# Attention heads taken in pairs: two halves of the array's rows for the logits, two halves of its columns for the weighted values

## The chip, the cores and the metric

The kernel runs on one core of a Trainium2 chip. A core has a matrix engine (TensorE, "PE" in the profile, its weight loads "PEld"), a vector engine (VectorE, "DVE"), an activation engine (ScalarE, "ACT"), a general engine (GpSimd, "POOL") and a queue engine (SyncE, "SP") that issues DMAs. TensorE multiplies a stationary operand, loaded into its array of 128 rows by 128 columns, with a moving operand that is streamed through it, and writes to PSUM, which has eight banks. The metric is the time of one execution in microseconds (us); smaller is better.

## What is computed

The reference is a transformer block (two kinds of attention, then a layer of product-key experts) followed by a second block. 256 tokens pass through both. The change lies in the attention of the first block alone: 16 heads of "forgetting" attention (fox) and 16 heads of "dilated" attention (dil), each head 64 wide. Cut to what matters:

```python
# fox: 16 heads of 64, S = 256, in two query blocks of 128
logits = einsum('bhqd,bhkd->bhqk', q * 64 ** -0.5, k) + (c[..., :, None] - c[..., None, :])
p = softmax(where(k_pos <= q_pos, logits, -inf))
o = einsum('bhqk,bhkd->bhqd', p, v)
...
# dil: three windows and dilations, mixed by their log-sum-exp; over 256 tokens this is
# one causal softmax whose logits get log(count) added, the count of patterns that hold the pair
out = concat([rms_norm(fox_o, fox_out_gain), rms_norm(dil_o, dil_out_gain)])
h = x + out @ w_out
```

The causal mask leaves 3 of 4 blocks of 128 by 128 logits for each head: block t = 0 has 128 keys, block t = 1 has 256.

## The kernel before, in words

All big products run in float32r (weights split into a high and a low half, three matmuls for each product), with weights streamed from memory: `Stream` brings 1 MB units by DMA, ACT rounds a half (line 74), DVE subtracts to get the low half (line 75), and PE uses it in `fm` (lines 105 to 107, 256 moving columns) or `tm` (lines 123 to 125, 512 moving columns). Splitting runs three halves ahead of the unit in use, with five half buffers.

The attention stage runs such products one after another: values, keys and queries of fox, then queries, keys and values of dil, then the output projection `w_out` in two halves of four chunks. Work of other kinds, the attention of single heads above all, is put between units of this stream: a list `k.bg` of steps, of which `pump` takes one after each unit (in the first half of `w_out` two in a row). The order on each engine is the program's order; no scheduler changes it.

`attention` makes 18 steps, and runs once for fox (on the units of `w_fq` and `w_dil`) and once for dil (on the last units of `w_dil` and on the first half of `w_out`). Step i holds three parts:

- `s1(i)`, the logits of head i: for fox a bias (line 278, two matmuls of 16 rows and 384 moving columns), then q times k (line 283: 64 rows, moving 128 and 256 columns, float32). An even head has rows 0 to 63 of the array, an odd head rows 64 to 127. Then the softmax: DVE reduces (line 289), ACT takes exp (line 293), DVE inverts and scales (lines 295 and 298) into the tile `lg`.
- `s3(i-1)`, three transposes of the probabilities of the head before (line 305), which ACT copies to `et` (line 307).
- `s4(i-2)`, the weighted values of the head before that (lines 316 and 317: 128 rows, 64 columns of the array, moving 256 and 128 columns, float32). An even head has columns 0 to 63, an odd head columns 64 to 127 of the same PSUM bank. After an odd head `on_pair` splits the pair's result (ACT line 221, DVE line 222), squares it (ACT line 450) and adds the square up (POOL line 451).

PSUM tiles of the tag `bg` rotate through four banks: one for a head's logits, one for its transposes, one for a pair's weighted values. Between these steps stands `rope_T` (line 509: eight transposes of rotated queries or keys, which wait for POOL's rotation, lines 496 to 501).

Of the kernel before, what the change touches and what calls it, by code (L numbers as in the profile page):

```python
# [9 lines left out]
F32 = mybir.dt.float32  # L10
# [5 lines left out]
AF = mybir.ActivationFunctionType  # L16
OP = mybir.AluOpType
# [8 lines left out]
BIG = 1e30  # L26
# [123 lines left out]
def bank(k, tag):  # L150
    return k.p_ps.tile([128, 512], F32, name=tag, tag=tag)
# [15 lines left out]
def pump(k, n=1):  # L167

    for _ in range(n):
        k.tick += 1  # L170
        for f in k.due.pop(k.tick, ()):
            f()
        if k.bg:
            k.bg.popleft()()
# [12 lines left out]
def step(us, f):  # L187
    f.us = us
    return f


def drain(k):
    while k.bg or k.due:
        pump(k)
# [19 lines left out]
def split(k, hi, lo, src, gain=None):  # L214

    nc = k.nc
    if gain is None:
        nc.scalar.copy(hi, src)
        nc.vector.tensor_sub(lo, src, hi.bitcast(F32))
    else:  # L220
        nc.scalar.mul(hi, src, gain)
        nc.vector.scalar_tensor_tensor(lo, src, gain, hi.bitcast(F32), op0=OP.mult, op1=OP.subtract)  # L222
# [44 lines left out]
def attention(k, bias, qT, kT, v, mask, on_pair):  # L267


    nc = k.nc  # L270
    E, ET, OTp = {}, {}, {}

    def s1(h):
        g, e = h // 2, (h % 2) * 64
        ps = bank(k, "bg")
        if bias:
            for i in range(2):
                nc.tensor.matmul(ps[:, :384], bias[1][:, h:h + 1].to_broadcast([16, 128]), bias[0][:, i, :],
                                 start=i == 0, stop=False)
        for t in range(2):  # L280
            o = ps[:, :128] if t == 0 else ps[:, 128:384]
            n = 128 * (t + 1)
            nc.tensor.matmul(o, qT[e:e + 64, g, t * 128:(t + 1) * 128], kT[e:e + 64, g, :n],
                             start=not bias, stop=not bias or t == 1)
        lg = k.p_at.tile([128, 384], F32, name="lg", tag="lg")
        st = k.p_at.tile([128, 6], F32, name="st", tag="st")
        for t in range(2):
            s = slice(0, 128) if t == 0 else slice(128, 384)
            nc.vector.tensor_tensor_reduce(lg[:, s], ps[:, s], mask[:, s], 1.0, BIG, op0=OP.add,
                                           op1=OP.min, accum_out=st[:, t:t + 1])  # L290
        for t in range(2):
            s = slice(0, 128) if t == 0 else slice(128, 384)
            nc.scalar.activation(lg[:, s], lg[:, s], AF.Exp, bias=st[:, t:t + 1], scale=-1.0,
                                 accum_out=st[:, 2 + t:3 + t])
        nc.vector.reciprocal(st[:, 4:6], st[:, 2:4])
        for t in range(2):
            s = slice(0, 128) if t == 0 else slice(128, 384)
            nc.vector.tensor_scalar_mul(lg[:, s], lg[:, s], st[:, 4 + t:5 + t])
        E[h] = lg

    def s3(h):
        ps = bank(k, "bg")
        e = E.pop(h)
        for b in range(3):
            nc.tensor.transpose(ps[:, b * 128:(b + 1) * 128], e[:, b * 128:(b + 1) * 128], k.ident)
        et = k.p_at.tile([128, 384], F32, name="et", tag="et")
        nc.scalar.copy(et, ps[:, :384])
        ET[h] = et

    def s4(h):  # L310
        g, e = h // 2, (h % 2) * 64
        et = ET.pop(h)
        if h % 2 == 0:
            OTp[g] = bank(k, "bg")
        o = OTp[g][e:e + 64, :256]
        nc.tensor.matmul(o, v[:, 0, h * 64:(h + 1) * 64], et[:, :256], start=True, stop=False)
        nc.tensor.matmul(o[:, 128:256], v[:, 1, h * 64:(h + 1) * 64], et[:, 256:384],
                         start=False, stop=True)
        if h % 2:
            on_pair(g, OTp.pop(g))  # L320

    def step(i):
        if i < 16:
            s1(i)
        if 0 <= i - 1 < 16:
            s3(i - 1)
        if 0 <= i - 2 < 16:
            s4(i - 2)
    return [lambda i=i: step(i) for i in range(18)]


def phase_attn(k, A):
    nc, st = k.nc, k.stream
    with ExitStack() as ctx:
# [41 lines left out]
        for c in range(2):  # L376
            accs = [[bank(k, ("acc", "bg")[c]) for t in range(2)] for s in range(2)]
            for q in range(4):
# [12 lines left out]
                for s in range(2):  # L391
                    tm(k, [a[:, :260] for a in accs[s]], w, k.act, q * 4, q == 0, q == 3,
                       n=260, off=s * 260, pitch=520, final=s == 1)
# [10 lines left out]
            for c in range(2):  # L404
                for s in range(2):
                    o = c * 520 + s * 260
                    n = min(260, 1024 - o)
                    for t in range(2):
                        acc = fv_acc[c][s][t]
                        nc.scalar.mul(fv[:, t, o:o + n], acc[:, :n], r[:, t:t + 1])  # L410
                        if n < 260:
                            nc.vector.scalar_tensor_tensor(zf[:, t, :], acc[:, n:260], r[:, t:t + 1],
                                                           fb, op0=OP.mult, op1=OP.add)
# [29 lines left out]
        def on_pair(o, sq, goff):  # L443
            def f(g, ps):
                split(k, o[0][:, g, :], o[1][:, g, :], ps[:, :256], k.gn[:, goff + g:goff + g + 1])
                if g == 0:
                    nc.scalar.activation(sq, ps[:, :256], AF.Square)
                else:
                    s = k.p_at.tile([128, 256], F32, name="sqt", tag="sqt")
                    nc.scalar.activation(s, ps[:, :256], AF.Square)  # L450
                    nc.gpsimd.tensor_add(sq, sq, s)
            return f
# [17 lines left out]
        for s in range(3):  # L470
            for c in range(2):
                accs = [bank(k, "acc") for t in range(2)]
                for q in range(4):
                    tm(k, accs, st.next(), k.act, q * 4, q == 0, q == 3)
                    if s == 2 and c == 0 and q == 2:
                        drain(k)
                        oD = [p1.tile([128, 8, 256], F32R, name="oD%d" % i, tag=("qkA", "qkB")[i]) for i in range(2)]
                        k.bg.extend(attention(k, None, dqT, dkT, dv, msk[:, M_D:M_D + 384],
                                              on_pair(oD, sqD, G_DIL)))
                    if q < 3:  # L480
                        pump(k)
                if s == 2:
                    for t in range(2):
                        nc.scalar.mul(dv[:, t, c * 512:(c + 1) * 512], accs[t], r[:, t:t + 1])
                    pump(k)
                    continue
                rp = k.p_at.tile([128, 2, 512], F32, name="rp", tag="rp", bufs=1)
                for t in range(2):
                    nc.scalar.mul(rp[:, t, :], accs[t], r[:, t:t + 1])
                for t in range(2):  # L490
                    hv = rp[:, t, :].rearrange("p (h e) -> p h e", e=64)
                    x1, x2 = hv[:, :, 0:8], hv[:, :, 8:16]
                    cb = cosv[:, t, None, :].to_broadcast([128, 8, 8])
                    sb = sinv[:, t, None, :].to_broadcast([128, 8, 8])
                    tt = [k.p_at.tile([128, 8, 8], F32, name="rt%d" % i, tag="rt%d" % i) for i in range(4)]
                    nc.gpsimd.tensor_mul(tt[0], x1, cb)
                    nc.gpsimd.tensor_mul(tt[1], x2, sb)
                    nc.gpsimd.tensor_mul(tt[2], x2, cb)
                    nc.gpsimd.tensor_mul(tt[3], x1, sb)
                    nc.gpsimd.tensor_sub(x1, tt[0], tt[1])  # L500
                    nc.gpsimd.tensor_add(x2, tt[2], tt[3])
                pump(k)

                def rope_T(rp=rp, c=c, dst=dkT if s == 1 else dqT, sc=1.0 if s == 1 else -0.125):
                    for q in range(2):
                        ps = bank(k, "bg")
                        for e in range(2):
                            for t in range(2):
                                nc.tensor.transpose(ps[:, e * 256 + t * 128:e * 256 + (t + 1) * 128],
                                                    rp[:, t, (q * 2 + e) * 128:(q * 2 + e + 1) * 128], k.ident)  # L510
                        nc.scalar.mul(dst[:, c * 4 + q * 2:c * 4 + q * 2 + 2, :].rearrange("p g t -> p (g t)"), ps, sc)
                k.bg.appendleft(rope_T)
# [12 lines left out]
        for half in range(2):  # L525
# [5 lines left out]
            o, rr = (oF, rF) if half == 0 else (oD, rD)  # L531
# [1223 lines left out]
```

## Time and profile before

| what | value |
|---|---|
| time, median of 3 runs | 2669.52 us (2668.6 to 2669.95) |
| the profiled execution's own time | 2668.61 us |
| its span on the core | 2666.8 us |
| PE busy | 2621.0 us (98%) |
| PE weight loads busy | 2395.4 us (90%) |
| DVE busy | 1850.6 us (69%) |
| ACT busy | 1438.8 us (54%) |
| POOL busy | 797.9 us (30%) |
| mean granted TensorE clock | 0.995 of full speed |

A float32 matmul stands in the trace as two records, here called passes, each with a weight load of its own; a transpose and a float32r matmul stand as one. The record of a matmul is longer than what it costs: records overlap, since the next one starts while the last one still drains. So time on PE is read here from the start of one row to the start of the next. In the timeline, rows of one line that follow each other are merged: the start of the first, the time to the end of the last, and "x" the number of passes.

### The profile page before, as it was taken

The numbers are of one execution on the slowest core, as the hardware profiler recorded it, in microseconds if no ns is written. First come the engines' busy times: TensorE is split into PE (matmuls) and PEld (weight loads), VectorE is DVE, ScalarE is ACT, GpSimd is POOL, SyncE is SP. The second block draws the span as 40 slices with busy tenths as digits, with TensorE's granted clock in tenths as the row PEclk, the third lists the DMA queues.
The fourth block names the chain that finished last, engine by engine and source line by source line (L and its number), as shares of the span: only waits on it lengthen the run. The fifth ranks groups of instructions, "written<-read, shape, count | busy, mean of one in ns | idle before, by whom it ended". The sixth has DMA issues, their size and how long they took to land. (4 is left out here: it accounts for less than half of the span.)

```text
span 2666.8 us, 45194 instructions
## 1 busy us (share of the span) xinstructions
PE 2621.0 (98%) x18008; PEld 2395.4 (90%) x18008; DVE 1850.6 (69%) x2679; ACT 1438.8 (54%) x2462; POOL 797.9 (30%) x858
## 2 busy tenths in 40 slices
PE   8999999999999999999999999999999999999997
PEld 8977778999999999999988888887999999999886
DVE  5554455799888899979856666665577765555555
ACT  6344455444466666647645555555665544444453
POOL 0001010432200033457645655634255530000000
PEclk9999999999999999999999999999999999999999
DMA  7533435446666688999968888775544446555553
GB/s 291 176 120 138 158 111 174 168 169 211 212 227 232 245 309 312 321 317 321 323 229 292 288 297 295 290 257 189 174 160 156 143 162 205 187 185 186 187 196 120
DMA packets 93975, 582.36 MB, mean 218 GB/s; under 512 B 12288, under 2 KB 12416, under 8 KB 32704
## 3 DMA queue, kind: packets, MB, share of 16 engines
q1 hardware_dynamic: 53696, 381.05, 41.1%
q0 software_dynamic: 35312, 183.46, 19.3%
q10 hardware_dynamic: 4752, 14.92, 1.5%
q8 instruction: 143, 2.34, 0.4%
q14 instruction: 72, 0.59, 0.1%
HBM read 532.19 MB, written 47.19 MB: 217 GB/s over the span
## 5 line engine op out<-in xcount | busy, mean ns | idle before, releaser
L75 DVE TENSOR_TENSOR whl<-raw,whl 128x1024 fp32r<-128x1024 f32 (+2 forms) x917 | 1186.2, 1306 | 585.3 <-ACT whl L74 560.9
L74 ACT CAST whl<-raw 128x1024 fp32r<-128x1024 f32 (+2 forms) x917 | 952.9, 1048 | 657.6 <-PE acc L107 330.9
L107 PE MATMUL acc<-act,whl 128*128 128x256 f32 x3840 | 1076.7, 280 | 3.5 <-DVE whl L75 3.5
L105 PE MATMUL acc<-act,whl 128*128 128x256 f32 x3840 | 1077.8, 281 | 0.2
L106 PE MATMUL acc<-act,whl 128*128 128x256 f32 x3840 | 1075.4, 280 | 0.4
L107 PEld LDWEIGHTS acc<-act,whl 128*128 128x128 f32 x3840 | 728.3, 190 | 3.9 <-DVE whl L75 3.9
L105 PEld LDWEIGHTS acc<-act,whl 128*128 128x128 f32 x3840 | 722.9, 188 | 2.3 <-issue 1.2
L106 PEld LDWEIGHTS acc<-act,whl 128*128 128x128 f32 x3840 | 723.6, 188 | 1.0 <-DVE act L222 1.0
L1160 PE MATMUL acc<-whl,hh 128*128 128x512 f32 x864 | 218.3, 396 | 0.0
L1160 PE MATMUL bg<-whl,hh 128*128 128x512 f32 x864 | 218.1, 396 | 0.0
L123 PE MATMUL acc<-whl,act 128*128 128x512 f32 (+1 forms) x512 | 198.3, 387 | 7.0 <-ACT whl L74 6.9
L124 PE MATMUL acc<-whl,act 128*128 128x512 f32 (+1 forms) x512 | 196.4, 384 | 4.1 <-DVE whl L75 4.1
L1160 PEld LDWEIGHTS bg<-whl,hh 128*128 128x128 f32 x864 | 162.2, 188 | 39.6
L1160 PEld LDWEIGHTS acc<-whl,hh 128*128 128x128 f32 x864 | 162.2, 188 | 39.5
L125 PE MATMUL acc<-whl,act 128*128 128x512 f32 (+1 forms) x512 | 196.1, 383 | 0.8 <-DVE act L222 0.8
L1085 POOL DMA_INDIRECT raw<-in_up,idx_l x100 | 137.0, 1370 | 136.6 <-DVE hh L911 76.9
L123 PEld LDWEIGHTS acc<-whl,act 128*128 128x128 f32 x512 | 97.7, 191 | 29.4 <-ACT whl L74 7.4
L124 PEld LDWEIGHTS acc<-whl,act 128*128 128x128 f32 x512 | 97.5, 190 | 24.7 <-DVE whl L75 5.9
L125 PEld LDWEIGHTS acc<-whl,act 128*128 128x128 f32 x512 | 97.4, 190 | 20.3 <-DVE act L222 1.0
L1085 POOL DMA_INDIRECT hr<-hm_d,idx_l x100 | 103.3, 1033 | 30.5 <-issue 30.5
L742 POOL DMA_DIRECT2D g_d<-gst x16 | 8.8, 551 | 291.9 <-DVE gst L726 291.9
L893 POOL TENSOR_TENSOR ght<-ght,gt 128x512 f32<-128x512 f32 x46 | 76.9, 1673 | 44.2 <-DMA ght<-gh_d 43.7
(405 smaller groups left out, 3176.1 us busy)
## 6 DMA issues: line engine op xcount, KB each, us to landing
raw<-in_down SPq DMA_DIRECT2D x128, 1024.0 KB, 5.8
raw<-in_w_cv SPq DMA_DIRECT2D x32, 1024.0 KB, 4.8
raw<-in_w_gg SPq DMA_DIRECT2D x32, 1024.0 KB, 4.8
raw<-in_w_dil SPq DMA_DIRECT2D x24, 1024.0 KB, 4.8
gt<-g_d POOLq DMA_DIRECT2D x34, 512.0 KB
raw<-in_w_out SPq DMA_DIRECT2D x16, 1024.0 KB, 4.8
raw<-in_w_pq SPq DMA_DIRECT2D x16, 1024.0 KB, 4.9
g_d<-gst POOLq DMA_DIRECT2D x16, 1024.0 KB
```

The source lines that it names most:

```text
L74: nc.scalar.copy(hi[:, s], r[:, s])
L75: nc.vector.tensor_sub(lo[:, s], r[:, s], hi[:, s].bitcast(F32))
L105: k.nc.tensor.matmul(acc, hi[:, f], x, start=j == 0, stop=False)
L106: k.nc.tensor.matmul(acc, hi[:, f], y, start=False, stop=False)
L107: k.nc.tensor.matmul(acc, lo[:, f], x, start=False, stop=j == nk - 1)
L123: k.nc.tensor.matmul(accs[t], ah[:, kk, ts], hi[:, m], start=st, stop=False)
L124: k.nc.tensor.matmul(accs[t], ah[:, kk, ts], lo[:, m], start=False, stop=False)
L125: k.nc.tensor.matmul(accs[t], al[:, kk, ts], hi[:, m], start=False, stop=sp)
L742: nc.gpsimd.dma_start(g_d[g], x.rearrange("p i t -> p (i t)"))
L893: nc.gpsimd.tensor_mul(x, x, gt[:, (j % 2) * 4:(j % 2) * 4 + 4])
L1085: nc.gpsimd.indirect_dma_start(out=out, out_offset=None, in_=table, in_offset=bass.IndirectOffsetOnAxis(ap=idx, axis=0), bounds_check=n - ...
L1160: nc.tensor.matmul(accs[2 * s + c][t], x[:, ts], y[:, c * 512:(c + 1) * 512], start=i == 0 and x is hh and y is hi, stop=last_ and i == N - 1)
```

## The change

`attention` now makes 19 steps over pairs g of heads (2g and 2g+1).

- An even step i = 2g takes the weighted values of pair g-2 (`outputs`) and then the logits of pair g (`logits`). An odd step i = 2g+3 takes the transposes of pair g (`turn`).
- In `logits` each head of the pair has a PSUM bank of its own. Both biases come first, then q times k of both heads for t = 0, then of both heads for t = 1, so that rows 0 to 63 and rows 64 to 127 alternate from one matmul to the next. The softmax of one head, then of the other, follows, operation by operation as before.
- In `outputs` both heads of the pair write to one bank as before; the two matmuls of 256 moving columns stand together, then the two of 128, so that columns 0 to 63 and columns 64 to 127 alternate.
- `lg` has four buffers in place of two. In return the tile `sqt` of `on_pair` and the four tiles `rt0` to `rt3` of the rotation have one buffer in place of two.

The number of matmuls, transposes and operations of the other engines is the same. Nothing outside the attention stage differs.

The new lines of `attention` (the lines that they replace are in the listing above) and the two changes of buffers:

```diff
+    E, ET = {}, {}
+    parts = (slice(0, 128), slice(128, 384))
+
+    def logits(g):
+
+        ps = [bank(k, "bg") for _ in range(2)]
+        if bias:
+            for e in range(2):
+                for i in range(2):
+                    nc.tensor.matmul(ps[e][:, :384], bias[1][:, 2 * g + e:2 * g + e + 1].to_broadcast([16, 128]),
+                                     bias[0][:, i, :], start=i == 0, stop=False)
+        for t in range(2):
+            for e in range(2):
+                es = slice(64 * e, 64 * e + 64)
+                nc.tensor.matmul(ps[e][:, parts[t]], qT[es, g, t * 128:(t + 1) * 128], kT[es, g, :128 * (t + 1)],
+                                 start=not bias, stop=not bias or t == 1)
+        for e in range(2):
+            lg = k.p_at.tile([128, 384], F32, name="lg", tag="lg", bufs=4)
...
+            E[2 * g + e] = lg
+
+    def turn(g):
+        for h in (2 * g, 2 * g + 1):
+            ps = bank(k, "bg")
+            e = E.pop(h)
+            for b in range(3):
+                nc.tensor.transpose(ps[:, b * 128:(b + 1) * 128], e[:, b * 128:(b + 1) * 128], k.ident)
+            ET[h] = k.p_at.tile([128, 384], F32, name="et", tag="et")
+            nc.scalar.copy(ET[h], ps[:, :384])
+
+    def outputs(g):
+
         ps = bank(k, "bg")
...
+        et = [ET.pop(2 * g + e) for e in range(2)]
+        for b, (o, s) in enumerate(((slice(0, 256), slice(0, 256)), (slice(128, 256), slice(256, 384)))):
+            for e in range(2):
+                h = 2 * g + e
+                nc.tensor.matmul(ps[64 * e:64 * e + 64, o], v[:, b, h * 64:(h + 1) * 64], et[e][:, s],
+                                 start=b == 0, stop=b == 1)
+        on_pair(g, ps)
 
     def step(i):
...
+        if i % 2 == 0:
+            if 0 <= i - 4 < 16:
+                outputs((i - 4) // 2)
+            if i < 16:
+                logits(i // 2)
+        elif 0 <= i - 3 < 16:
+            turn((i - 3) // 2)
+    return [lambda i=i: step(i) for i in range(19)]
...
-                    s = k.p_at.tile([128, 256], F32, name="sqt", tag="sqt")
+                    s = k.p_at.tile([128, 256], F32, name="sqt", tag="sqt", bufs=1)
...
-                    tt = [k.p_at.tile([128, 8, 8], F32, name="rt%d" % i, tag="rt%d" % i) for i in range(4)]
+                    tt = [k.p_at.tile([128, 8, 8], F32, name="rt%d" % i, tag="rt%d" % i, bufs=1) for i in range(4)]
```

How this moves PE's work shows in the order of its instructions. In fox, while `w_fq` and `w_dil` stream, PE has between two units before, for each head (`cT` and `id_131` make the bias, `fkT` and `fqT` are keys and queries, `cst` is the identity, `lg` the probabilities, `et` their transposes, `fv` the values, `acc` rows are the stream's):

```order
L107 MATMUL acc<-act_81,whl 128x256
L278 MATMUL bg<-cT,id_131 128x384 x2
L283 MATMUL bg<-fkT,fqT 128x128
L283 MATMUL bg<-fkT,fqT 128x256
L305 MATMUL bg<-cst,lg 128x128 x3
L316 MATMUL bg<-et,fv 64x256
L317 MATMUL bg<-et,fv 64x128
L105 MATMUL acc<-act_81,whl 128x256
```

And with the change, at the same place, for each pair (the new lines are 280 for the bias, 285 for q times k, 306 for the transposes, 317 for the weighted values):

```order
L317 MATMUL bg<-et,fv 64x256 x2
L317 MATMUL bg<-et,fv 64x128 x2
L280 MATMUL bg<-cT,id_131 128x384 x4
L285 MATMUL bg<-fkT,fqT 128x128 x2
L285 MATMUL bg<-fkT,fqT 128x256 x2
L123 MATMUL acc<-whl,act_81 128x512
...
L306 MATMUL bg<-cst,lg 128x128 x6
```

The row of 128 columns and that of 64 columns, which stood once between any two units, now stand twice in a row between every second two, and the transposes have a place of their own between units.

In dil, on the first half of `w_out`, where two steps run in a row (`dkT`, `dqT`, `dv` are keys, queries and values), PE has before:

```order
L283 MATMUL bg<-dkT,dqT 128x128
L283 MATMUL bg<-dkT,dqT 128x256
L305 MATMUL bg<-cst,lg 128x128 x3
L316 MATMUL bg<-et,dv 64x256
L317 MATMUL bg<-et,dv 64x128
```

twice over between two units, and with the change once:

```order
L125 MATMUL acc<-whl,oF_674 128x512
L317 MATMUL bg<-et,dv 64x256 x2
L317 MATMUL bg<-et,dv 64x128 x2
L285 MATMUL bg<-dkT,dqT 128x128 x2
L285 MATMUL bg<-dkT,dqT 128x256 x2
L306 MATMUL bg<-cst,lg 128x128 x6
L123 MATMUL acc<-whl,oF_673 128x512
```

The weighted values moved ahead of the logits, and the transposes behind them.

## Rows read from the trace of the kernel before

**Rows 1.** The page: span, and each engine's busy time, share and instructions.

```profile
span 2666.8 us, 45194 instructions
PE 2621.0 (98%) x18008; PEld 2395.4 (90%) x18008; DVE 1850.6 (69%) x2679; ACT 1438.8 (54%) x2462; POOL 797.9 (30%) x858
```

**Rows 2.** Attention stage: us; PE, PEld, DVE, ACT, POOL busy (instructions); clock; DMA share; GB/s.

```profile
113.00:413.00 300.00, 299.94 (x1497) 228.61 (x1496) 152.66 (x333) 144.96 (x289) 31.56 (x74) 1.00 0.39 135
```

**Rows 3.** Waits of PE's weight loads, 113 to 413 us: us, times, longest.

```profile
PEld bg L509 <- POOL rp L501: 0.4, 1, 0.4
```

**Rows 4.** Timeline of PE, one fox step: start, us, engine, line, operation, passes.

```profile
130.11 0.28 PE L107 MATMUL acc<-act,whl 128*128 128x256 f32 x1
130.32 0.61 PE L278 MATMUL bg<-cT,id 16*128 16x384 f32 x2
130.86 0.92 PE L283 MATMUL bg<-fkT,fqT 64*128 64x128 f32 x4
131.71 0.55 PE L305 MATMUL bg<-cst,lg 128*128 128x128 f32 x3
132.19 0.65 PE L316 MATMUL bg<-et,fv 128*64 128x256 f32 x2
132.67 0.38 PE L317 MATMUL bg<-et,fv 128*64 128x128 f32 x2
132.98 0.39 PE L105 MATMUL acc<-act,whl 128*128 128x256 f32 x1
133.20 0.28 PE L106 MATMUL acc<-act,whl 128*128 128x256 f32 x1
133.32 0.28 PE L107 MATMUL acc<-act,whl 128*128 128x256 f32 x1
```

**Rows 5.** Timeline of PE: eight transposes between matmuls of 128 rows and columns.

```profile
206.22 1.03 PE L509 MATMUL bg<-cst,rp 128*128 128x128 f32 x8
...
207.33 0.39 PE L124 MATMUL acc<-whl,act 128*128 128x512 f32 x1
```

**Rows 6.** Timeline of PE's weight loads, the same fox step.

```profile
130.86 0.52 PEld L283 LDWEIGHTS bg<-fkT,fqT 64*128 64x128 f32 x4 [0.25 <-issue]
...
132.18 0.19 PEld L316 LDWEIGHTS bg<-et,fv 128*64 128x64 f32 x2 [0.17 <-issue]
```

**Rows 7.** Timeline of PE: two dil steps in a row.

```profile
349.47 0.40 PE L124 MATMUL acc<-whl,oF 128*128 128x512 f32 x1
349.70 0.40 PE L125 MATMUL acc<-whl,oF 128*128 128x512 f32 x1
350.03 0.92 PE L283 MATMUL bg<-dkT,dqT 64*128 64x128 f32 x4
...
353.00 0.64 PE L305 MATMUL bg<-cst,lg 128*128 128x128 f32 x3
...
354.71 0.39 PE L124 MATMUL acc<-whl,oF 128*128 128x512 f32 x1
```

**Rows 8.** Timeline of all engines: dil's last two heads, one after the other.

```profile
401.02 0.48 ACT L307 COPY et<-bg 128x384 f32<-128x384 f32 x1 [2.12 <-PE bg L305]
...
401.34 0.38 PE L317 MATMUL bg<-et,dv 128*64 128x128 f32 x2
401.55 0.19 PEld L316 LDWEIGHTS bg<-et,dv 128*64 128x64 f32 x2
401.55 0.65 PE L316 MATMUL bg<-et,dv 128*64 128x256 f32 x2
```

**Rows 9.** Timelines of DVE and ACT: softmax of one dil head, and a pair's end.

```profile
350.99 0.29 DVE L289 CUSTOM_DVE_ANT_0 lg<-bg,amsk 128x128 f32<-128x128 f32 x1 [1.27 <-PE bg L283]
...
353.11 0.29 DVE L289 CUSTOM_DVE_ANT_0 lg<-bg,amsk 128x128 f32<-128x128 f32 x1
...
354.75 0.47 ACT L221 ACTIVATE oD<-bg,gn 128x256 fp32r<-128x256 f32 x1
355.84 0.39 ACT L450 ACTIVATE sqt<-bg 128x256 f32<-128x256 f32 x1 [0.61 <-DVE oD L222]
```

More of the change, by code (lines that the diff above doesn't have):

```diff
@@ L270, in attention @@
     nc = k.nc
-    E, ET, OTp = {}, {}, {}
-    def s1(h):
-        g, e = h // 2, (h % 2) * 64
-        ps = bank(k, "bg")
[L276 to L320, printed above, removed]
@@ L322, in step @@
-    def step(i):
[L323 to L329, printed above, removed]
+    E, ET = {}, {}
[14 more added lines that the diff above has]
+            lg = k.p_at.tile([128, 384], F32, name="lg", tag="lg", bufs=4)
+            st = k.p_at.tile([128, 6], F32, name="st", tag="st")
+            for t, s in enumerate(parts):
+                nc.vector.tensor_tensor_reduce(lg[:, s], ps[e][:, s], mask[:, s], 1.0, BIG, op0=OP.add,
+                                               op1=OP.min, accum_out=st[:, t:t + 1])
+            for t, s in enumerate(parts):
+                nc.scalar.activation(lg[:, s], lg[:, s], AF.Exp, bias=st[:, t:t + 1], scale=-1.0,
+                                     accum_out=st[:, 2 + t:3 + t])
+            nc.vector.reciprocal(st[:, 4:6], st[:, 2:4])
+            for t, s in enumerate(parts):
+                nc.vector.tensor_scalar_mul(lg[:, s], lg[:, s], st[:, 4 + t:5 + t])
+            E[2 * g + e] = lg
```

## The prediction

> **What bounds the kernel now.** I read the page first: PE is busy for 98% of the span, but its records overlap, so that alone proves little [rows 1]. The busy times of the attention stage, 113 to 413 us, say more: PE 299.94 of 300 us at a granted clock of 1.00, DVE and ACT half idle, the DMAs at 0.39 [rows 2]. In the list of waits of the same stretch no matmul of attention waits for another engine by more than some tenths; the one wait with a cause outside attention is 0.4 us for POOL's rotation [rows 3]. So PE's own sequence sets the pace there, and what shortens it should shorten the run. The timeline gives the price of that sequence, read from start to start.
>
> A fox step costs 133.20 - 130.11 - 2 x 0.12 = 2.85 us beyond the stream's matmuls (spaced 0.12) [rows 4]. Its parts come out with three prices:
>
> - A float32 pass of 128 moving columns takes 0.11 us: the eight transposes take 207.33 - 206.22 less one matmul of the stream (0.23), and 0.88 / 8 = 0.11 [rows 5, 7]. One of 256 takes 0.215: (132.67 - 132.19 - 0.05) / 2, where 0.05 is a weight load of 64 columns, from two loads of some 0.14 within 0.19 [rows 4, 6].
> - Weight loads of 128 columns follow each other by 0.11: four in 0.52, the last 0.19 long [rows 6]. Within a group they hide under the pass before.
> - Where the shape of the tile used changes (all rows, 16 rows, 64 rows, 64 columns), the next group starts 0.09 late (from 130.11 to 130.32 is 0.21, against 0.12), and its first weight load is no longer hidden: 0.11 for 128 columns, 0.05 for 64 columns and for a transpose [rows 4, 6]. The eight transposes among the stream's matmuls, of the same shape, pay neither [rows 5].
>
> With these the step is 0.09 + 0.54 (bias) + (0.11 + 0.22 + 0.43 + 0.09) + (0.05 + 0.33 + 0.09) + (0.05 + 0.43 + 0.22 + 0.09) + 0.10 = 2.83, against 2.85 read: 1.95 of passes and 0.90 for five changes of shape.
>
> **What the change removes.** Passes stay the same in number. Changes of shape become fewer. In fox two steps pay 10 for a pair, 1.80 us. After it, the even step pays columns (0.14), 16 rows (0.21), 64 rows (0.20) and back (0.19), together 0.74; the transposes stand alone among matmuls of their own shape and pay nothing. That is 1.06 us for a full pair. Counted step by step, since the ends of the pipeline differ: before, 14 full steps at 0.90 and the first and last two at 0.60, 0.55, 0.33 and 0.33, together 14.4; after, six full even steps at 0.74, two with logits alone at 0.60 and two with outputs alone at 0.33, together 6.3. Saved: **8.1 us**.
>
> In dil there is no bias. Before: two first steps (0.39, 0.34), four single ones at 0.67, five double ones at 1.15 and the last at 0.33, together 9.5. After: two logits steps at 0.39, one with both at 0.53, five double ones at 0.14 + 0.20 + 0.14 = 0.48, then 0.28 and 0.33, together 4.3. Saved 5.2. As a test, a double step by these prices is 2 x 1.63 + 1.15 = 4.41; the trace has 354.71 - 349.70 - 2 x 0.23 = 4.55 [rows 7]. The surplus is in the second transposes (0.64 us for three, where fox shows 0.55): they need the softmax of the head whose logits have just run [rows 4, 7]. Afterwards that softmax has a unit of the stream to finish in. Five of these, 0.1 each: 0.5. Dil saves **5.7 us**, and both together 13.8.
>
> **What the change adds.** The two halves of the array now alternate, a thing that the trace never shows with data ready. A pair's q times k is 8 passes, 4 x 0.11 + 4 x 0.215 = 1.30 us one after the other; the weighted values of a pair are 1.30 too. Bounds: they add up as before (saving 0), or passes of one half run beside those of the other. Each matmul is two passes in the same half, and PE starts in program order, so only the second pass of one head can run beside the first of the next: 8 parts of 0.108 in place of 12, a saving of 0.43 for either block. For the rows the weight loads are a limit: eight of 128 columns, 0.11 apart, as long as the short passes themselves, which leaves 10 parts of 12, a saving of 0.21. Loads of 64 columns, 0.05 apart, limit nothing [rows 6].
>
> The nearest row is at the end of dil, where the weighted values of head 14 (columns 0 to 63) and of head 15 (64 to 127) follow each other [rows 8]. The last pass of the first starts at 401.34 + 0.11 = 401.45 and streams until 401.56; the weight load of the other half starts at 401.55, just after its data came (the copy ends at 401.02 + 0.48 = 401.50). A change of shape would have held it until 401.65. So a change of half doesn't drain the array, and a load goes into one half while the other streams. Whether two halves also stream together it doesn't show, since the data came too late. I take it that they do, because nothing but the order of starts ties them, and take the lower figure for the rows: 0.43 + 0.21 = 0.64 a pair, 16 pairs, **10.2 us**. Ends: 0 and 16 x 0.86 = 13.8.
>
> [...]
>
> **What hides the rest.** On DVE and ACT the operations are the same, in another order: two softmaxes in a row, 2 x (353.11 - 350.99) = 4.2 us [rows 9], in which DVE does no splitting of weights. Splits are three halves, over 8 us of PE, ahead, and DVE's mean load is half, so this costs nothing. The probabilities are wanted a full unit (5.5 us) later. In dil's double steps the second head's transposes need the bank of the weighted values just written, free after ACT's split, DVE's and the square: 355.84 + 0.39 - 354.75 = 1.5 us [rows 9], plus 0.3 to start. PE covers 0.2 + 0.2 + 1.3 + 0.14 + 0.33 without overlap, 1.9 or 1.7 with it; at worst 0.2 x 5 = 1 us, which I leave to the range. A rotation before which only transposes stand has 0.66 us more time than the one that waited 0.4 [rows 3], so it adds no wait. The single buffers for `sqt` and `rt` are taken again on the same engine, or two units later: nothing.
>
> **The sum.** 13.8 + 10.2 = 24.0 us. The profiled execution took 2668.6 (span 2666.8 and 1.8 around it), 0.9 under the median of 2669.5. So 2644.6 on its own time, **2645.5** for the median.
>
> **Rivals.** *The halves don't stream together* (the change doesn't do what it says): only the shape changes are saved, 2669.5 - 13.8 = 2655.7. For it: no row shows two float32 passes at once. Against: the load into the other half. *Only one block overlaps*: columns alone 2648.8, rows alone 2652.3. *Both halves stream all the time*: each block falls from 1.30 to 0.65, which saves 13.8 + 16 x 1.30 = 34.6 and gives 2634.9; against it speaks that the two passes of a matmul share their half and that PE starts in order. [...] *Slower: each alternation drains as a change of shape does.* Three in the rows at 0.20 and three in the columns at 0.14 make 1.02 us a pair, 16.3 in all, against the 13.8 saved: 2672.0, slower than before. It decides from 13.8 / 96 = 0.14 us for an alternation. Rows 8 speak against it for the columns; for the rows nothing is shown, and there alone it would be 9.6 us, not enough to lose. For this to reach beyond measurement, waits of other engines must come on top.
>
> **How the numbers follow.** Overlap in both, 24 to 27.6 us: 0.50. One block only: 0.14. None: 0.26. Full halves: 0.03. Draining halves: 0.05. Waits that nobody saw: 0.02. The range runs from full overlap, 2641.9 less 3 us for prices read to 0.01 us, to no overlap, 2655.7 plus 1 us for the banks: 2639 to 2657, holding the first three. A measurement of this kernel can tell about 0.2%, 5.3 us: faster by more 0.93 (the first four cases), the same 0.05, slower 0.02.
>
> **What would show it.** In the timeline of the changed kernel a full fox pair, outputs and logits together, should take 4.0 us without overlap and 3.4 with it, and its transposes 0.66. Overlap shows in the starts: the first pass of the second head beside the second pass of the first, and the block of lines 285 and 317 shorter than 1.3 us. If the starts of line 285 lie 0.2 apart at each change of head, the halves drain. PE should still have no wait on DVE or ACT; a wait of the transposes for line 450 would make the prediction too low. It is wrong as a whole if another engine, freed of nothing, turns out to hold PE back once PE needs 8% less time in this stage.

## The result and the profile after

The changed kernel takes 2633.6 us (2632.74 to 2634.49), against 2669.06 of the kernel before in the same runs; the ratio is 0.9876, interval 0.9864 to 0.9887. That is 35.5 us less, where 24 were forecast, and 5.4 us below the range. The direction was right, the size was not.

The page of the changed kernel shows the same work in a shorter span (against [rows 1]):

```profile
span 2630.9 us, 45199 instructions
PE 2585.7 (98%) x18008; PEld 2378.6 (90%) x18008; DVE 1846.4 (70%) x2679; ACT 1439.2 (55%) x2462; POOL 788.4 (30%) x858
```

The stage that was 113 to 413 us [rows 2] now ends at 381.4. Busy time by stretch, columns as there (PE, PEld, DVE, ACT, POOL, clock, DMA share, GB/s):

```profile
113.00:381.40 268.40, 267.15 (x1498) 214.00 (x1497) 149.42 (x333) 144.86 (x289) 33.57 (x74) 1.00 0.44 151
```

It holds the same operations, 31.6 us shorter, and PE is still what never stops: 267.15 of 268.40 us.

Where the time went is in the timeline of PE, for a pair of fox heads (start, us, engine, line, operation, passes; [rows 4] has the same for one head):

```profile
142.66 0.28 PE L107 MATMUL acc<-act,whl 128*128 128x256 f32 x1
142.87 0.87 PE L317 MATMUL bg<-et,fv 128*64 128x256 f32 x8
143.67 0.96 PE L280 MATMUL bg<-cT,id 16*128 16x384 f32 x4
144.55 0.93 PE L285 MATMUL bg<-fkT,fqT 64*128 64x128 f32 x8
145.41 0.38 PE L105 MATMUL acc<-act,whl 128*128 128x256 f32 x1
145.63 0.28 PE L106 MATMUL acc<-act,whl 128*128 128x256 f32 x1
```

Read from start to start: the eight passes of q times k take 145.41 - 144.55 = 0.86, of which 0.11 is the first weight load and 0.09 the way out. That leaves 0.66 for passes that are 1.30 one after the other. The weighted values take 143.67 - 142.87 = 0.80, less 0.05 and 0.09: 0.66 again. Both blocks are at half. The whole step costs 145.63 - 142.66 - 2 x 0.12 = 2.73 us where 3.4 was forecast with overlap.

How they come to half shows where a window is opened on the first 0.1 us of the weighted values alone, PE and its weight loads:

```profile
142.86 0.20 PEld L317 LDWEIGHTS bg<-et,fv 128*64 128x64 f32 x4
142.87 0.44 PE L317 MATMUL bg<-et,fv 128*64 128x256 f32 x2
```

Two passes together last 0.44 us, no longer than one record alone (0.43), so they are the first passes of the two heads, and start within 0.01 us of each other; four weight loads fit in 0.20. The prediction had let only the second pass of one head run beside the first of the next.

One place got worse, and eats 2.2 us. In dil's double steps PE now waits for a bank (timeline of all engines, beside [rows 7] and [rows 9]):

```profile
325.94 0.87 PE L317 MATMUL bg<-et,dv 128*64 128x256 f32 x8
...
326.74 0.93 PE L285 MATMUL bg<-dkT,dqT 64*128 64x128 f32 x8
326.86 0.47 ACT L221 ACTIVATE oD<-bg,gn 128x256 fp32r<-128x256 f32 x1 [2.50 <-PE bg L317]
327.37 0.48 DVE L222 SCALAR_TENSOR_TENSOR oD<-bg,gn,oD 128x256 fp32r<-128x256 f32 x1 [1.73 <-ACT oD L221]
...
327.60 0.55 PE L306 MATMUL bg<-cst,lg 128*128 128x128 f32 x3
...
327.95 0.38 ACT L450 ACTIVATE sqt<-bg 128x256 f32<-128x256 f32 x1 [0.61 <-DVE oD L222]
...
328.38 0.31 PEld L306 LDWEIGHTS bg<-cst,lg 128*128 128x128 f32 x3 [0.48 <-ACT sqt L450]
```

The second head's transposes need the bank that held the pair's weighted values; split, subtraction and square read it one after the other until 328.33, and the transposes start at 328.38. In the list of waits of 113 to 385 us this is the largest with a cause:

```profile
PEld bg L306 <- ACT sqt L450: 2.4, 5, 0.5
...
PEld bg L509 <- POOL rp L501: 0.8, 2, 0.4
```

### The profile page after: what moved, and what is told of

Its sections match the earlier page's. It is cut to its first block, busy times and chain, and to the rows that moved or that the text cites. A ratio compares the mean times of both kernels' runs of the same rounds, so it can differ in the third digit from the quotient of the medians.

```text
span 2630.9 us, 45199 instructions
## 1 busy us (share of the span) xinstructions
PE 2585.7 (98%) x18008; PEld 2378.6 (90%) x18008; DVE 1846.4 (70%) x2679; ACT 1439.2 (55%) x2462; POOL 788.4 (30%) x858
## 5 line engine op out<-in xcount | busy, mean ns | idle before, releaser
L1085 POOL DMA_INDIRECT raw<-in_up,idx_l x100 | 130.1, 1301 | 145.4 <-DVE hh L911 78.0
```

The costliest lines, as they stand in the source:

```text
L1085: nc.gpsimd.indirect_dma_start(out=out, out_offset=None, in_=table, in_offset=bass.IndirectOffsetOnAxis(ap=idx, axis=0), bounds_check=n - ...
```

## The experiments

Unless said otherwise, each is an edit of the changed kernel, and is compared with its attention stage: steps of 2.74 us (fox, even), 0.66 (transposes alone) and 2.92 (dil, double), each beyond the stream's own matmuls.

**Do the halves matter, or only the order?** The logits of both heads on the same rows:

```diff
-                es = slice(64 * e, 64 * e + 64)
+                es = slice(0, 64)
```

> The changed kernel, but the logits of both heads of a pair are taken from rows 0 to 63 (so the odd head's logits are those of the even head: that part of the computation is left out). Order, banks and sizes unchanged. If the gain of the block is the two halves of the rows, q times k takes 8 passes one after the other, 1.30 us in place of 0.65: 16 x 0.65 = 10.4 us more, less the wait of dil's double steps (0.43 x 5 = 2.2): 2641.8. Rival (two banks or the alternation of independent matmuls suffice): 0.65 as before, 2633.6.

Measured: 2643.74 us (2640.91 to 2649.53), 2641.8 expected. Timeline of PE, a pair of fox heads:

```profile
146.45 0.96 PE L280 MATMUL bg<-cT,id 16*128 16x384 f32 x4
147.34 1.57 PE L285 MATMUL bg<-fkT,fqT 64*128 64x128 f32 x8
148.84 0.39 PE L105 MATMUL acc<-act,whl 128*128 128x256 f32 x1
```

The block takes 1.50 us in place of 0.86, so the eight passes take 1.30, the sum that the prediction had for no overlap. Two banks and alternating matmuls give nothing; two halves of the rows give all of the block's gain. Double steps come to 3.12, not 2.92 + 0.64: the longer block hides the wait for the bank again. The rival falls. The columns have no such run of their own. For them the evidence is the timeline: the same bank is written before and after, and the eight passes take 0.66 in place of 1.30.

**Does the order matter?** Both blocks head by head, without alternation:

```diff
-        for t in range(2):
-            for e in range(2):
+        for e in range(2):
+            for t in range(2):
...
-        for b, (o, s) in enumerate(((slice(0, 256), slice(0, 256)), (slice(128, 256), slice(256, 384)))):
-            for e in range(2):
+        for e in range(2):
+            for b, (o, s) in enumerate(((slice(0, 256), slice(0, 256)), (slice(128, 256), slice(256, 384)))):
```

> The changed kernel with both blocks written head by head: both matmuls of head 2g (t = 0, 1 or the two of the weighted values), then both of head 2g+1. Same pairs, same number of shape changes, no alternation. In the trace of the changed kernel an alternating block of eight passes takes 0.65 us. Theory A (each half of the array runs its own matmul with its two passes; matmuls are handed out in program order, and one waits only for its own half): q times k 0.22 + 0.22 + 0.43 = 0.87, weighted values 0.43 + 0.43 + 0.22 = 1.08 us; the wait of dil's double steps (0.43 x 5) goes: 2633.6 + 16 x 0.65 - 2.2 = 2641.8. Rival B (a queue for each half, order without weight): blocks stay 0.65, 2633.6. Rival C (passes in program order, as the prediction had it): 1.08 and 1.19, 2633.6 + 16 x 0.97 - 2.2 = 2647. Rival D (no overlap without alternation): 1.30 each, 2652.

Measured: 2635.7 us (2634.67 to 2639.17); the attention stage ends at 382.20, against 381.96 with alternation. The block of line 285 is as long as there:

```profile
144.55 0.93 PE L285 MATMUL bg<-fkT,fqT 64*128 64x128 f32 x8
145.42 0.38 PE L105 MATMUL acc<-act,whl 128*128 128x256 f32 x1
```

My theory fell, and so did the order of passes that the prediction rested on: rival B is right. The first passes of the two heads, though two matmuls apart in the program, start 0.013 us apart (0.006 with alternation). A window on the first 0.05 us of the block shows two passes here, and one in same_rows, where both heads use one half:

```profile
144.55 0.39 PE L285 MATMUL bg<-fkT,fqT 64*128 64x128 f32 x2
```

```profile
147.34 0.37 PE L285 MATMUL bg<-fkT,fqT 64*128 64x128 f32 x1
```

So in headwise a matmul that waits for its own half (the first head's second) doesn't hold up the one behind it that has the other half.

**How far ahead?** headwise, with the second matmul of each head cut into four of 64 columns, so that five matmuls (ten passes) of one head stand ahead of the other's:

```diff
-                nc.tensor.matmul(ps[e][:, parts[t]], qT[es, g, t * 128:(t + 1) * 128], kT[es, g, :128 * (t + 1)],
-                                 start=not bias, stop=not bias or t == 1)
+                w = 128 if t == 0 else 64
+                for j in range(128 * (t + 1) // w):
+                    o = parts[t].start + w * j
+                    nc.tensor.matmul(ps[e][:, o:o + w], qT[es, g, t * 128:(t + 1) * 128], kT[es, g, w * j:w * j + w],
+                                     start=not bias, stop=not bias or o + w == 384)
```

> headwise, with the second matmul of each head's logits (256 columns) cut into four of 64, so that five matmuls, ten passes, of the even head stand ahead of the first of the odd head. How far ahead does PE find work for the idle half? Theory A (far enough for these): the odd head's first pass starts within 0.05 us of the even head's; with a weight load of 0.11 for each pass the block takes 2 x 0.11 + 8 x 0.11 = 1.1 us. Rival B (a short look ahead, of two matmuls as headwise needed): the odd head starts after some of the even head's passes, and the block takes 1.5 to 2.2 us. Rival C (weight loads of the two halves share one path): 20 loads of 0.11, 2.2 us whatever the order.

One run: 2653.88 us. The block in the timeline, and then the busy time and count of these matmuls (line 288 here) in its first 0.74 us and in the next 0.40, with clock and DMA (a record that only reaches into a stretch is counted in it too):

```profile
146.22 2.05 PE L288 MATMUL bg<-fkT,fqT 64*128 64x128 f32 x20
148.20 0.39 PE L105 MATMUL acc<-act,whl 128*128 128x256 f32 x1
```

```profile
146.20:146.94 0.74, 0.71 (x6) 1.00 0.87 365
146.94:147.34 0.40, 0.40 (x10) 1.00 1.01 430
```

The block is 1.98 - 0.09 = 1.89 us long, between full overlap (1.1) and none (2.2). In its first 0.74 us there are six passes, one half's own pace; the other head's first pass starts at 146.95, when the fourth of the first head's five matmuls has just started. So it runs ahead of one matmul that hasn't started, the fifth. In headwise it is the same: there one matmul of the first head has started, and one hasn't. That reach was enough for two matmuls and isn't for five; what alternation in the program would give with five, no run shows. Rival B again; rival C (one path for both halves' loads) is ruled out by the alternating kernel already, with four loads in 0.20 us.

The whole time of this run holds something else besides. Within its attention stage the granted clock fell to 0.50 four times for 3.4 us, each time 0.6 to 0.9 us after one of the eight long blocks of fox (its mean over the run is 0.993); over the same stage it reads 1.00 in the kernel before, in the changed kernel and in the run best below. PE in the first of these stretches:

```profile
164.70:168.10 3.40, 3.40 (x10) 0.50 0.01 2
```

The stream's matmuls stand 0.43 us apart in it and 0.23 behind it, which makes some 1.6 us a stretch and 6 in all (an estimate from these spacings). The blocks themselves are read at full clock.

**Is the bank the wait, and can it be had back?** First, the logits ahead of the weighted values in the even step, so that another bank comes round:

```diff
-            if 0 <= i - 4 < 16:
-                outputs((i - 4) // 2)
             if i < 16:
                 logits(i // 2)
+            if 0 <= i - 4 < 16:
+                outputs((i - 4) // 2)
```

> The changed kernel with logits(g) ahead of outputs(g-2) in the even step; nothing else differs. Theory: in dil's double steps the second head's transposes wait 0.4 to 0.5 us for the bank of the weighted values, which the square of line 450 frees last (five waits, 2.4 us in the trace). With the logits first, the fifth bank taken in a step is that of the first head's logits, which DVE frees 0.7 us after the logits while PE still has the weighted values and three transposes: the waits of line 306 for line 450 go, a double step falls from 2.92 to 2.5, and the time to 2633.6 - 2.1 = 2631.5. Rival (PE waits for ACT or DVE as such, which are late by the softmax): the wait moves to another row, 2633.6 or more.

Measured: 2638.11 us (2636.09 to 2640.67), where 2631.5 was expected; the attention stage ends 3.1 us later than the changed kernel's (385.06 against 381.96). The waits for line 450 are gone, and the first double step falls to 2.47 us as expected; the next ones take 3.23, 3.83, 3.56 and 3.56. Timeline of DVE and then of PE, the third double step:

```profile
344.19 2.36 DVE L75 TENSOR_TENSOR whl<-raw,whl 128x1024 fp32r<-128x1024 f32 x2 [1.17 <-ACT whl L74]
346.47 0.28 DVE L291 CUSTOM_DVE_ANT_0 lg<-bg,amsk 128x128 f32<-128x128 f32 x1
```

```profile
345.48 0.55 PE L306 MATMUL bg<-cst,lg 128*128 128x128 f32 x3
347.17 0.55 PE L306 MATMUL bg<-cst,lg 128*128 128x128 f32 x3 [1.14 <-DVE st L291]
```

The bank that comes round now waits for DVE's first reduction of the logits, and DVE reaches that late: the pair's split and square stand behind the softmax on ACT and DVE, the weight splits behind them, and so two subtractions of weights (line 75) run on DVE when the logits are ready. The rival is right about what comes next, the theory about the bank. The double steps make 2.0 of the 3.1 us; another 1.0 is a longer wait for POOL's rotation in fox (1.7 in all, where it was 0.8, by the lists of waits), whose cause no run shows. Then the same aim without moving anything behind the softmax: the pair's values are copied out of PSUM once, and split and square read the copy.

```diff
-                split(k, o[0][:, g, :], o[1][:, g, :], ps[:, :256], k.gn[:, goff + g:goff + g + 1])
+                s = k.p_at.tile([128, 256], F32, name="sqt", tag="sqt", bufs=1)
+                nc.scalar.copy(s, ps[:, :256])
+                split(k, o[0][:, g, :], o[1][:, g, :], s, k.gn[:, goff + g:goff + g + 1])
...
-                    nc.scalar.activation(sq, ps[:, :256], AF.Square)
+                    nc.gpsimd.tensor_mul(sq, s, s)
...
-                    s = k.p_at.tile([128, 256], F32, name="sqt", tag="sqt", bufs=1)
-                    nc.scalar.activation(s, ps[:, :256], AF.Square)
+                    nc.gpsimd.tensor_mul(s, s, s)
```

> The changed kernel, but on_pair copies the pair's weighted values from PSUM once (ACT, some 0.38 us), and the split (ACT, DVE) and the square (now a product on POOL) read the copy. The bank of the weighted values is then free 1 us earlier. Theory: line 306's wait for that bank (five of 0.5 in dil's double steps) goes without putting anything on DVE behind the softmax: a double step falls from 2.92 to 2.5 and the attention stage by 2.1 us, 2631.5. Rival (as in logits_first: the next wait in line, DVE's reduction or POOL, takes its place): double steps of 2.9 or more, 2633.6 or later. What POOL gets more (16 products of some 0.75 us) may hold the rotation back in fox, at most 0.4 us in each of 4 places.

Measured: 2633.13 us (2631.03 to 2635.86), the stage 2.3 us shorter (379.66 against 381.96). All five double steps take 2.47 us, and the six transposes run through:

```profile
326.75 0.93 PE L285 MATMUL bg<-dkT,dqT 64*128 64x128 f32 x8
327.60 0.87 PE L306 MATMUL bg<-cst,lg 128*128 128x128 f32 x6
328.23 0.48 PE L123 MATMUL acc<-whl,oF 128*128 128x512 f32 x1
```

The theory holds: 5 x 0.45 = 2.2 us were the bank.

**Does it go beyond halves?** Fox's bias, 16 rows, held a second time at rows 32 to 47, and the two heads alternating between the two places (the cumulative sums are formed twice, in two groups of columns, with copies and splits to match):

```diff
-            for e in range(2):
-                for i in range(2):
-                    nc.tensor.matmul(ps[e][:, :384], bias[1][:, 2 * g + e:2 * g + e + 1].to_broadcast([16, 128]),
-                                     bias[0][:, i, :], start=i == 0, stop=False)
+            for i in range(2):
+                for e in range(2):
+                    p = slice(32 * e, 32 * e + 16)
+                    nc.tensor.matmul(ps[e][:, :384], bias[1][p, 2 * g + e:2 * g + e + 1].to_broadcast([16, 128]),
+                                     bias[0][p, i, :], start=i == 0, stop=False)
...
-        cT = p1.tile([16, 2, 384], F32R, name="cT")
+        cT = p1.tile([48, 2, 384], F32R, name="cT")
```

> The changed kernel with fox's bias in two row groups: the 16 rows of the bias and its selector are held twice, at rows 0 to 15 and 32 to 47, and the two heads alternate between them. Theory A (any two groups of rows run side by side, 32-row ones too): four bias passes of 0.175 take the time of two, 0.35 us less for each of 8 pairs, 2.8 in all, against some 0.7 us for the doubled cumulative sums once: 2631.5. Rival (only halves of 64 run side by side): no gain, 0.7 us more, 2634.3.

Measured: 2632.56 us (2629.95 to 2634.2). The bias now takes 144.85 - 144.31 = 0.54 us for a pair, where it took 144.55 - 143.67 = 0.88:

```profile
144.31 0.62 PE L281 MATMUL bg<-cT,id 16*128 16x384 f32 x4
144.85 0.93 PE L286 MATMUL bg<-fkT,fqT 64*128 64x128 f32 x8
```

Two groups of 16 rows, at 0 and at 32, run side by side as well. The doubled cumulative sums cost PE nothing, where I had feared 0.7 us: they too run side by side, in two groups of 16 columns. From their first pass to the stream's next matmul it is 0.76 us in both kernels, with 6 passes in the changed kernel and 12 here:

```profile
69.94 0.39 PE L430 MATMUL bg<-cst,fz_b 128*16 128x128 f32 x2
...
70.70 0.39 PE L105 MATMUL acc<-act,whl 128*128 128x256 f32 x1
```

```profile
71.50 0.40 PE L433 MATMUL bg<-cst,fz_b 128*16 128x128 f32 x4
...
72.26 0.39 PE L105 MATMUL acc<-act,whl 128*128 128x256 f32 x1
```

**The price of a change of shape, by itself.** free_bank with the transposes between weighted values and logits, the odd step left empty:

```diff
             if 0 <= i - 4 < 16:
                 outputs((i - 4) // 2)
+            if 0 <= i - 2 < 16:
+                turn((i - 2) // 2)
             if i < 16:
                 logits(i // 2)
-        elif 0 <= i - 3 < 16:
-            turn((i - 3) // 2)
```

> free_bank with the transposes moved: outputs(g-2), turn(g-1) and logits(g) all in the even step, the odd step empty. No matmul more or less, but a change of shape more: from columns to transposes 0.09 + 0.05, where it went straight to the next. Theory: fox's full even step takes 2.74 + 0.66 + 0.14 = 3.54 us, a double step of dil 2.47 + 0.19 = 2.66 (the transposes no longer stand beside the stream's matmuls of their own shape). Rival (a change of shape costs nothing beyond the load that it exposes, 0.05): 3.45 and 2.6. A wait of the odd head's logits for the bank of the weighted values would come on top.

One run: 2639.46 us. Fox's full even step takes 3.55 us, dil's double step 2.66, against 3.54 and 2.66 expected:

```profile
142.76 0.28 PE L107 MATMUL acc<-act,whl 128*128 128x256 f32 x1
142.97 0.87 PE L317 MATMUL bg<-et,fv 128*64 128x256 f32 x8
143.77 0.88 PE L306 MATMUL bg<-cst,lg 128*128 128x128 f32 x6
144.58 0.96 PE L280 MATMUL bg<-cT,id 16*128 16x384 f32 x4
145.47 0.93 PE L285 MATMUL bg<-fkT,fqT 64*128 64x128 f32 x8
146.33 0.39 PE L105 MATMUL acc<-act,whl 128*128 128x256 f32 x1
146.55 0.28 PE L106 MATMUL acc<-act,whl 128*128 128x256 f32 x1
```

The transposes take 144.58 - 143.77 = 0.81 here and 0.66 among matmuls of their own shape. The 0.15 between them is the 0.05 on the way in and 0.09 on the way out as priced, to 0.01; how it divides between the two isn't shown.

**The rest of the span.** The attention stage explains 31.6 us of the 35.9 by which the two profiled executions differ. The remaining 4.3 lie behind it, where no instruction has changed. The changed kernel once more:

> The changed kernel unaltered, beside more runs of the kernel before. In the first traces the attention stage ends 31.7 us earlier, and the rest of the span, whose instructions are the same, is 4 us shorter. Theory A (the rest varies from run to run with waits in the expert stage and with short dips of the granted clock): the rest comes out elsewhere within 2247 to 2254 us, and the medians differ by 32 to 36. Theory B (the earlier end does something for the rest): the rest is again near 2249, and the medians differ by 35 to 36.

Measured: 2636.56 us (2634.87 to 2640.41) against 2665.15 of the kernel before in these runs, ratio 0.9891, 0.9874 to 0.9907. The rest of the span, from the sum of squares behind attention to the end, in the kernel before, the changed kernel and the changed kernel again (PE busy and its count, clock, DMA; the third row has all engines):

```profile
413.50:2666.80 2253.30, 2215.70 (x15659) 0.99 0.65 228
```

```profile
381.90:2630.90 2249.00, 2214.10 (x15659) 0.99 0.65 229
```

```profile
382.10:2636.20 2254.10, 2216.30 (x15659) 2063.79 (x15658) 1629.41 (x2257) 1235.97 (x2087) 754.17 (x780) 0.99 0.66 228
```

On the rest theory A holds and B falls: 2249 the first time, 2254 the second, 2253 before, and in the other variants 2247.6 to 2255.5, somewhat beyond the range that A gave. Of the 5.1 us between the two profiles of the changed kernel 2.2 are in PE's busy time and 2.9 in its idle time. On the medians both theories missed: they differ by 28.6, below the 32 to 36 of A. The attention stage of the changed kernel, by contrast, ends at 381.96 and 382.17. So the change itself is worth 31.6 us, and a comparison of medians gives that with 3 to 4 us of the rest on top or below (35.5 and 28.6).

**A version that beats both.** free_bank and bias_two together:

> free_bank and bias_two together: double steps of dil 2.5 in place of 2.92 (2.1 us), fox's even steps 2.40 in place of 2.74 (2.7 us). If both are pure PE time and nothing else becomes late, 2633.6 - 4.8 = 2628.8, faster than the kernel before and the changed one. Rival: ACT and DVE now set the pace of the double steps, no more than bias_two alone.

Measured: 2627.97 us (2626.07 to 2631.85), ratio to the kernel before 0.9855, 0.9839 to 0.9872; 8.6 us under the changed kernel in the same runs. Its attention stage ends 5.5 us earlier than that one's (376.66 against 382.17), 4.8 expected, so the rival falls; the other 3 us of the medians are within the spread of the rest.

## Why the prediction was right and wrong

- *PE's own sequence sets the pace.* Right: PE busy for 267.15 of 268.40 us after the change, and the gains in the blocks went through to the end of the stage (bias_two and free_bank together: 4.8 expected, 5.5 measured). The list behind [rows 3] holds three more waits with a releaser outside attention (0.4, 0.3 and 0.2 us), which the prediction passed over; they are too short to change the sum.
- *Changes of shape, 13.8 us.* Right, as far as the runs show: they weren't measured by themselves as a sum, but of the stage's 31.6 us the overlap (20.6) and the new waits (2.2) leave 31.6 - 20.6 + 2.2 = 13.2. A full fox even step without overlap was put at 4.00; it measures 2.74 plus the 1.29 that overlap saves. The transposes alone take 0.66, as said, and turn_between prices a change at 0.15 in fox and 0.19 in dil where 0.14 and 0.19 were reckoned. The wait of dil's transposes for the softmax, 0.5 in all, is gone.
- *Overlap, 10.2 us (ends 0 and 13.8).* This is the step that failed. It measures 16 x 1.29 = 20.6. Two assumptions were wrong. The first, that "PE starts in program order", so that only the second pass of a head meets the first of the next: [rows 4] has lines 278, 283, 305, 316 and 317 start in the program's order, but no row shows that order for two halves with data ready, and headwise shows that a matmul blocked on its half is passed by one for the other half (the other head's first pass starts 0.013 us after the first head's, ahead of a matmul that stands before it in the program). The second, that weight loads of 0.11 follow one another whichever half they go to: four loads of two halves take 0.20 us, the time of two (0.19), and the eight of line 285 take 0.52, the time of four [rows 6]. The rival of full halves, at 0.03, was the case, and its 34.6 less the bank waits of 2.2 is what the stage shows, to within 0.8. The upper bound was set by these two, and no row of before bears on either: it has no two matmuls on different halves with data ready, and the loads of [rows 6] all go to one half. So the bound should have been the full half, and the range should have reached 2634.
- *The bank of the weighted values, at worst 1 us.* The place was right, the size wrong: the wait is 0.45 in each of five steps. What has to be covered was as said: 328.33 - 326.86 = 1.47 us against 1.5, and 0.3 to start. The cover was not. The prediction's terms for it add up to 2.17, not to the 1.9 that it gives, and with blocks at half they are 0.2 + 0.2 + 0.65 + 0.14 + 0.33 = 1.52. The trace leaves less still: from ACT's start at 326.86 to the time when the first three transposes are through, 327.60 + 0.33 = 327.93, it is 1.07, with the 0.3 to start 1.37.
- *The rotation adds no wait.* Nearly: 0.8 us in two places, where it was 0.4 in one [rows 3].
- *The rest of the span stays.* It moved by some 4 us of its own, which the prediction had no room for. With the kernel's own spread, the range would have missed in either run: 2633.6 and 2636.6 both lie under 2639.

## What to carry to other kernels

Where PE sets the pace and small matmuls stand among large ones, count the changes of shape: each cost here the way out (0.09 us) and a first weight load that nothing hid (0.05 to 0.11), so collect work of one shape before going back. Matmuls on half of the array's rows or columns came two for one here (0.66 us for 1.30) where a partner for the other half, with its data ready, had one matmul of the first half ahead of it (the changed kernel) or two (headwise); with five ahead (headwise_deep) the block took 1.89, where full overlap was reckoned at 1.1. Strict alternation wasn't needed, being near was. When PE gets faster in a block, look at which buffer comes round in that time, and free it by one copy (free_bank: the stage 2.3 us shorter) rather than by moving work behind something longer (logits_first: 3.1 us longer).

## What the hardware showed that was not expected

- Two halves of the array took weight loads and passes at once, with starts within 0.013 us of each other, and the pair took no longer than one (0.66, for 1.30 one after the other). This held for halves of rows and halves of columns (0.66 for either block), for two groups of 16 rows at 0 and 32 (0.54 for 0.88), and for two groups of 16 columns (12 passes in the 0.76 of 6).
- A matmul ran ahead of one that stands before it and waits for its own half, but in both runs that show it (headwise, headwise_deep) it ran ahead of one only: with five of one half in front, the other half started 0.72 us late.
- A change of half cost nothing that shows: the block of line 285 takes 0.86 us with three of them and 0.87 with one (headwise). A change of shape cost 0.15 us in fox and 0.19 in dil where it was measured by itself (turn_between), and 0.14 to 0.21 by the prices read from [rows 4] and [rows 6].
- In the profile of the kernel before, the granted clock fell to half for 3.4 us within 468 to 474 us, where PE had just waited six times, 1.8 us in all, for the split of the activations (lines 221 and 222). At the same place, with the same waits, it stayed at full in the first profile of the changed kernel and fell in the second, so the change isn't its cause. PE alone, before, after, and after again:

```profile
468.00:474.00 6.00, 5.73 (x29) 0.72 0.60 203
```

```profile
436.00:442.00 6.00, 5.72 (x41) 1.00 0.54 187
```

```profile
436.20:442.20 6.00, 5.73 (x27) 0.72 0.59 189
```

  29 and 27 passes with the dip, 41 without: such a dip costs some 1.5 us (an estimate: 12 to 14 passes, 0.12 apart). It is a part of what the rest of the span varies by, but not of the 4.3 us between the first two profiles: behind attention, up to the last 15 us, each of these has 13.6 us at half clock.
